# A decoder layer on one core: token blocks loaded and summed between the index logits, the index keys in another buffer, and the second token block's attention scores from halves

## The chip, the core and the metric

The kernel runs on one core of a Trainium2 chip. The core has TensorE (PE, matrix products, with its weight loads shown apart as PEld), VectorE (DVE), ScalarE (ACT), GpSimd (POOL) and SyncE (SP, which issues most DMA transfers). Each engine works through its own instructions in order; semaphores make one wait for another. Products are written to banks of PSUM, a small memory that DVE and ACT read; everything else lies in SBUF. The metric is the device time of one execution in microseconds (us).

## What is computed

One layer: a projection of x into ten parts, retention over four heads, sparse attention over four heads in which an indexer picks the 128 best keys of each query, an output projection with a layer norm, and a gated feed-forward block with another norm. There are 512 tokens and a model width of 1024.

```python
def hybrid_layer(x, positions, w_in, ret_gn_gain, w_out, ...):
    proj = x @ w_in
    rq, rk, rv, rg, aq, ak, av, iq, ik, iw = jnp.split(proj, IN_SPLITS, axis=-1)
    rq = rope(rq); rk = rope(rk); aq = rope(aq); ak = rope(ak); iq = rope(iq); ik = rope(ik)
    ret = silu(rg) * group_norm(retention_chunkwise(rq, rk, rv))
    # indexer: which keys may a query see
    logits = relu(einsum('bqhd,bsd->bqhs', iq, ik))
    score = where(key <= query, einsum('bqh,bqhs->bqs', iw, logits), -inf)
    sel = top_k(score, 128)
    # attention over the chosen keys alone
    s = einsum('bqhd,bkhd->bhqk', aq, ak) * 128 ** -0.5
    att = softmax(where(sel, s, -inf)) @ av
    mix = concatenate([ret, att]) @ w_out
    x = layer_norm(ALPHA * x + mix, ...)
    gate, up = jnp.split(x @ w_gate_up, 2)
    return layer_norm(ALPHA * x + (silu(gate) * up) @ w_down, ...)
```

(Reshapes and chunk loops are left out, and `rope` and the norm are abbreviated.)

## The kernel before

**Numbers in halves.** Most products are made from float32 numbers split into a rounded part of type fp32r and the rest, called hi and lo or h and l. `mm3` (lines 93 to 96) makes hi·hi, hi·lo and lo·hi in three products. `split` makes the parts: ACT casts the hi part (L86), and DVE or POOL subtracts it from the source (L91), or ACT negates it (L88) and a DMA issued by POOL adds the source in memory (L89). Some products are made directly from float32 numbers: transposes, retention's, and the attention scores of the token blocks 0 and 1 (L695).

**Stages.** Tokens lie in four blocks of 128. First the index parts of the projection are made (`acc`), then eight column groups of ak, aq, rk and rq (`proj_feature`, products named `pf`, sixteen of 24 products each), then rv and rg together (`token_pair`), which makes them by seven block products instead of eight. For that it needs sums of blocks of x: block "11" holds the first half of the tokens and the first half of the width, and so on; `x_load` fetches two of these by DMA, `x_sums` forms s3, s1, n2 and s4 by four subtractions and additions on POOL (L394), and `x_split` splits them into halves. Then `proj_token` makes av (products `pt`), with retention beside it. Then `mix_part` makes the output projection (products `mx`), with attention beside it. The feed-forward block comes last.

**Side work.** Beside the products of each stage runs side work that generators deliver: `pace` calls them at a given rate. The list `side` holds, one behind the other, the rotary work of the index parts, the logits (`logits`: two products per head of the indexer, a relu on ACT, L502, and a weighted sum on DVE, L508), and the top-k search (`topk`: 16 times MAX8 and MATCH_REPLACE8 on DVE, L519 and L520, per token block). `both` mixes logits and top-k steps. `slots` runs `mix_part` and, behind each of its sixteen groups of three products, what a plan names for that slot; behind that it steps the side work. `weight()` hands out the next split weight and prepares the one three ahead, so a call of it puts a cast on ACT (`wh`) and a subtraction (`wl`) on DVE or POOL.

**Attention.** `att_score(b)` is a generator of three steps: the scores of four heads, each in a bank of PSUM, and DVE's reading of them, with the mask added and the row maximum taken (L697, L699); then the exponentials on ACT (L702, with the load of ACT's table ahead of the first); then the division by the sum on DVE (L705, L707). `att_tr` transposes the result by PE (L716, tile `apt`) and ACT copies it (L718); `att_pv` multiplies by the values. `ak_split` and `aq_split` make the halves of keys and queries for the blocks 2 and 3; `ak_split` takes a pair of heads at a time. Line 968 makes the scores of block 1 ahead of `mix_part(0, 0)`.

**Buffers.** PSUM has four banks with the tag "d" (`psd`, accumulators) and four with the tag "u" (`psu`, all else: logits, scores, transposes). A new tile of a tag waits until an older one has been read. The large SBUF buffers have tags as well (`s0` to `s10`, `X0` to `X3`), and a new tile of a tag waits for all users of the one before. The index keys `kk3` lie in s8, which the blocks "11" and "22" take after them; rqT lies in s3.

Of the kernel before, what the change touches and what calls it, by code (L numbers as in the profile page):

```python
# [53 lines left out]
def hybrid_layer_kernel(ctx: ExitStack, tc: tile.TileContext, xT, x, pos, w0, wf, wt, wo,  # L54
# [21 lines left out]
    def unit(tag, name, dt=F32):  # L76
        return big.tile([P, 4, S], dt, tag=tag, name=name)
# [142 lines left out]
    def rope(dst, src, ct, st, lo=0, held_back=False):  # L220
        t1 = tmp("rt1")
        t2 = tmp("rt2")
        n = slice(lo, S)
        V.tensor_tensor(t1[:, n], src[:, n], ct[:, n], op=ALU.mult)
        V.tensor_tensor(t2[0:64, n], src[64:128, n], st[64:128, n], op=ALU.mult)
        V.tensor_tensor(t2[64:128, n], src[0:64, n], st[0:64, n], op=ALU.mult)
        if dst is not None:
            late.append(lambda: G.tensor_tensor(dst, t1[:, n], t2[:, n], op=ALU.add))
            if not held_back:
                late.pop()()  # L230
        return t1, t2
# [2 lines left out]
    qa = big.tile([P, 4, M], F32R, tag="s4", name="qa")  # L234
    qb = big.tile([P, 4, M], F32R, tag="s5", name="qb")
    ql = big.tile([P, 4, M], F32R, tag="s6", name="ql")
    kk3 = big.tile([P, 3, S], F32R, tag="s8", name="kk3")
    kh, kl = kk3[:, 0], (kk3[:, 1], kk3[:, 2])
    iwr = tmp("iwr")
    iw = const.tile([P, NB, IH], F32, name="iw")  # L240
# [1 line left out]
    def index_rope():  # L242
        G.memset(kk3[:, 1:].bitcast(F32), 0.0)
        A.activation(iwr, acc0[0], AF.Copy, scale=IDX_SCALE)
        t1, t2 = rope(None, acc0[0], CI, SI)
        ks = tmp("ks")
        V.tensor_tensor(ks, t1, t2, op=ALU.add)
        yield 1.7

        def halves_k():  # L250
            A.copy(kh, ks)
            for b in (0, 64):
                s, d = slice(b, b + 32), slice(b + 32, b + 64)
                G.tensor_tensor(kl[0][s], ks[s], kh[s].bitcast(F32), op=ALU.subtract)
                nc.gpsimd.dma_start(kl[1][d].bitcast(F32), kl[0][s].bitcast(F32))
                nc.gpsimd.dma_start(kh[d].bitcast(F32), kh[s].bitcast(F32))

        def halves_q(i, qs):
            A.copy(qa[:, i], qs[:, P:])
            A.copy(qb[:, i], qs[:, P:])  # L260
            G.tensor_tensor(ql[:, i], qs[:, P:], qa[:, i].bitcast(F32), op=ALU.subtract)
            if i % 2:
                n = slice(i - 1, i + 1)
                for d, s in ((qa[32:64, n], ql[0:32, n]), (qa[96:128, n], ql[64:96, n]),
                             (qb[0:32, n], ql[32:64, n]), (qb[64:96, n], ql[96:128, n])):
                    nc.gpsimd.dma_start(d.bitcast(F32), s.bitcast(F32))

        rounding = halves_k
        for i in range(4):
            t1, t2 = rope(None, acc0[1 + i], CI, SI, P)  # L270
            qs = tmp("qs")
            V.tensor_tensor(qs[:, P:], t1[:, P:], t2[:, P:], op=ALU.add)
            rounding()
            rounding = lambda i=i, qs=qs: halves_q(i, qs)
            yield 2.3
        rounding()
        yield 3.0
        iwp = psu("iwp")
        for j in range(1, NB):
            T.transpose(iwp[:, j * P:(j + 1) * P], iwr[:, j * P:(j + 1) * P], ident)  # L280
        A.copy(iw[:, 1:], iwp.rearrange("p (j c) -> p j c", c=P)[:, 1:, 32:32 + IH])
        yield 3.0
# [36 lines left out]
    akT = unit("s0", "akT")  # L319
    aqT = unit("s1", "aqT")  # L320
    rkT = unit("s2", "rkT")
    rqT = unit("s3", "rqT")
    feats = [akT, aqT, rkT, rqT]
    gnb = const.tile([P, S], F32, name="gnb")

    def const_loads():
# [10 lines left out]
    def dense(items, evac, group=8):  # L337
        for n, item in enumerate(items):
            item()
            if n == 0:  # L340
                settle()
            if n % group == group - 1 or n == len(items) - 1:
                yield
        pending.append(evac)

    def proj_feature(c):
        for i in range(2):
            h, l = weight()
            acc = psd(f"pf{c}_{i}")

            def items(acc=acc, h=h, l=l):
                for kt in range(KT):
                    cs = slice(kt * P, kt * P + P)
                    yield lambda cs=cs, kt=kt: mm3(acc, h[:, cs], l[:, cs], xh[kt], xl[kt], kt == 0, kt == KT - 1)

            yield from dense(list(items()), lambda i=i, acc=acc: rope(feats[c // 2][:, 2 * (c % 2) + i], acc, CT, ST, 0, (c, i) == (7, 1)), 3)

    tok = {}

# [25 lines left out]
    def x_load(tag, *names):  # L385
        t = big.tile([P, 2, 4, T2], F32, tag=tag, name=f"xq{tag}")
        for i, q in enumerate(names):
            tok_half, k_half = int(q[0]) - 1, int(q[1]) - 1
            dma(t[:, i], xT[4 * k_half:4 * k_half + 4, :, T2 * tok_half:T2 * tok_half + T2].rearrange("k p c -> p k c"))
            xq[q] = t[:, i]  # L390
# [134 lines left out]
    def chain(*its):  # L525
        for it in its:
            yield from it
# [44 lines left out]
    def heads(t):  # L572
        return t.rearrange("p (h c) -> p h c", c=P)
# [4 lines left out]
    def ret_score(b):  # L578
        bs = slice(b * P, b * P + P)
        if b:  # L580
            rt["q", b] = tmp(f"rqd{b}")
            G.tensor_tensor(heads(rt["q", b]), rqT[:, :, bs], heads(rt["decay"][:, 1]), op=ALU.mult)
        sc = psu(f"rs{b}")
        for h in range(HEADS):
            T.matmul(sc[:, h * P:h * P + P], lhsT=rkT[:, h, bs], rhs=rqT[:, h, bs], start=True, stop=True)
        rt["s", b] = tmp(f"rst{b}")
        V.tensor_tensor(rt["s", b], sc, rt["decay"][:, 0], op=ALU.mult)

# [67 lines left out]
    def retention():  # L656
        steps = (((ret_keys, 0),), ((ret_score, 0),), ((ret_keys, 1),), ((ret_state, 0),), ((ret_score, 1), (ret_decay, 1)), ((ret_out, 0, 0),),
                 ((ret_out, 0, 1),), ((ret_state, 1),), ((ret_keys, 2),), ((ret_score, 2), (ret_decay, 2)), ((ret_out, 1, 0),),
                 ((ret_out, 1, 1), (ret_scale, 0)), ((ret_state, 2),), ((ret_score, 3), (ret_scale, 1), (gated, 0)), ((ret_out, 2, 0), (ret_gate, 0)),
                 ((ret_out, 2, 1), (gated, 1)), ((ret_out, 3, 0), (gated, 2), (ret_gate, 1)), ((ret_out, 3, 1), (gated, 3)), ((ret_turn, 0), (ret_scale, 2)),  # L660
                 ((ret_gate, 2),), ((ret_turn, 1),), ((ret_scale, 3),), ((ret_gate, 3), (ret_turn, 2)), (), (), ((ret_turn, 3),), ())
        for step in steps:
            for f, *a in step:
                f(*a)
            yield
# [2 lines left out]
    at = {}  # L668
    ak2, aq2 = [], {}

    def ak_split(pair):
        if not ak2:
            ak2.extend(big.tile([P, 4, S], F32R, tag=t, name=f"ak_{t}") for t in ("s7", "s6"))
        hs = slice(2 * pair, 2 * pair + 2)
        A.copy(ak2[0][:, hs], akT[:, hs])
        for h in (2 * pair, 2 * pair + 1):
            G.tensor_tensor(ak2[1][:, h], akT[:, h], ak2[0][:, h].bitcast(F32), op=ALU.subtract)

    def aq_split(b):
        hi, lo = aq2[b] = [tmp(f"aq{i}{b}", F32R) for i in "hl"]  # L680
# [54 lines left out]
    const_loads()  # L735
    tk = chain(*[topk(j) for j in range(1, NB)])

    def x_parts():
        x_load("s8", "11", "22")
        yield 0.01  # L740

    def some(it, n):
        for _ in range(n):
            yield next(it)

    def splits(*a):
        if a[0] == "s4":
            drain(sums_it)
        x_split(*a)
        yield 0.5  # L750

    def x_sums_in():
        next(sums_it)
        next(sums_it)
        yield 0.01

    def both(main, it, every):
        for n, c in enumerate(main):
            yield c
            if n % every == every - 1:  # L760
                yield next(it)

    sums_it = x_sums()
    lg1, lg23 = logits(1), chain(logits(2), logits(3))
    side = chain(index_rope(), lg1, both(lg23, tk, 2), x_parts(), some(tk, 3), x_sums_in(), some(tk, 3), splits("s1", "s4"), some(tk, 1), splits("s4", "s6"), tk)
    run(chain(*[proj_feature(c) for c in range(4)]), pace(side, 1.0))
    x_load("s10", "21", "12")
    run(chain(*[proj_feature(c) for c in range(4, 7)]), pace(side, 1.4))
# [146 lines left out]
    def slots(main, plan, *sides):  # L915
        for n, _ in enumerate(main):
            for f in plan.get(n, ()):
                f()
            for s in sides:
                next(s, None)  # L920
# [15 lines left out]
    def sc_(b):  # L936
        return lambda: next(sc[b])
# [22 lines left out]
    def gate_(n):  # L960
        def f():
# [3 lines left out]
        return f  # L965

    settle()
    sc_(1)()
    slots(mix_part(0, 0), {1: trs_(0, 0), 2: [lambda: ak_split(1)], 6: [lambda: aq_split(2)], 10: [lambda: aq_split(3)], 3: [*trs_(0, 2), *pvs_(0, 0), sc_(1), sc_(1)], 5: pvs_(0, 2), 9: trs_(1, 0),
                           11: [*trs_(1, 2), *pvs_(1, 0)], 13: pvs_(1, 2), 15: [sc_(2)]}, pace(side, 0.5))  # L970
    drain(side)
    slots(mix_part(0, 1), {0: [sc_(2)], 2: [sc_(2)], 3: [sc_(3)], 4: [gate_(0)], 5: trs_(2, 0), 6: [sc_(3)], 7: [*trs_(2, 2), *pvs_(2, 0)],
# [916 lines left out]
```

## Time and profile before

| | |
|---|---|
| median of 3 executions | 606.54 us (606.04 to 606.6) |
| profiled execution | 606.31 us |
| its span, from the first to the last instruction | 604.5 us |
| mean granted clock of TensorE | 0.998 |
| HBM read and written | 90.25 MB and 2.10 MB |

The profile is of one execution, and its rows give start and length in us from the start of the span. A row of the timeline stands for one or several equal instructions (x8) and says in brackets how long the engine sat idle before and which instruction of which engine ended that. The ends of matrix products are modelled and overlap, so their pace is read from start to start. A matrix product of float32 numbers leaves two records.

### The profile page before, as it was taken

The page shows a single profiled execution, that of the slowest core. Times are in us where ns is not written, and L with a number is a line of the kernel's source. Part 1 is how long each engine was busy: PE and PEld are TensorE (multiplying, and loading weights), DVE is VectorE, ACT ScalarE, POOL GpSimd, SP SyncE. Part 2 cuts the span into 40 slices and gives each one's busy share as a digit, 9 for nine tenths or more (in the row PEclk, how much of TensorE's full clock was granted, in tenths as well). Part 3 has the DMA queues.
Part 4 walks back from the last instruction along what each step waited for, and adds up shares of the span by engine and source line. Part 5 has one row for each costly group of instructions (what it writes and reads, how often), then busy time and mean ns, then how long its engine had stood idle before and what let it go on. Part 6 is the DMA issues. An engine that isn't in the chain of part 4 may idle for free.

```text
span 604.5 us, 9142 instructions
## 1 busy us (share of the span) xinstructions
PE 595.5 (99%) x3212; PEld 515.5 (85%) x3212; DVE 528.2 (87%) x975; ACT 367.3 (61%) x640; POOL 196.0 (32%) x196
## 2 busy tenths in 40 slices
PE   9999999999999999999999999999999999999995
PEld 7988888888888888889998888888888888888884
DVE  6896698999958888989998999999999899999856
ACT  5645555445584956777756777777676795547300
POOL 1188323967866400342222222232221021201010
PEclk9999999999999999999999999999999999999999
DMA  8889888699794771696598988988887469678302
GB/s 303 299 217 256 215 208 234 157 240 215 186 225 162 270 266 70 154 227 127 143 274 181 255 191 229 248 198 232 187 224 187 127 189 233 168 243 271 90 36 105
DMA packets 43822, 121.52 MB, mean 201 GB/s; under 512 B 4560, under 2 KB 11536, under 8 KB 38144
## 3 DMA queue, kind: packets, MB, share of 16 engines
q1 hardware_dynamic: 25024, 82.00, 40.2%
q0 software_dynamic: 17872, 36.64, 34.1%
q10 hardware_dynamic: 880, 2.29, 1.2%
q8 instruction: 25, 0.41, 0.3%
q14 instruction: 21, 0.17, 0.1%
HBM read 90.25 MB, written 2.10 MB: 153 GB/s over the span
## 4 chain that ended last, share of the span: by engine, by line
PE 94%; DMA 4%; ACT 1%; issue 1%; DVE 1%; POOL 0%; DVEq 0%; POOLq 0%; ACTq 0%
PE ga L1107 16%; PE gc L1107 8%; PE pf L94 5%; PE pf L95 5%; PE pf L96 5%; PE gb L1107 4%; PE acc L210 4%; PE ga L1097 4%; PE dl L95 2%; PE dl L96 2%; PE dl L94 2%; PE gc L1097 2%; PE dr L95 2%; PE dr L94 2%; PE dr L96 2%; DMA part<-kept 2%
## 5 line engine op out<-in xcount | busy, mean ns | idle before, releaser
L86 ACT CAST wh<-raw 128x1024 fp32r<-128x1024 f32 x49 | 51.2, 1050 | 30.1 <-DMA raw<-in_wt_dram 8.3
L94 PE MATMUL pf<-xh,wh 128*128 128x512 f32 x128 | 50.0, 391 | 0.0
L95 PE MATMUL pf<-xl,wh 128*128 128x512 f32 x128 | 49.9, 390 | 0.0
L96 PE MATMUL pf<-xh,wl 128*128 128x512 f32 x128 | 49.8, 389 | 0.0
L557 POOL TENSOR_TENSOR rs<-ve,half 128x1 f32<-128x1 f32 (+1 forms) x11 | 13.8, 1252 | 74.9 <-DVE ve L556 74.9
L91 DVE TENSOR_TENSOR wl<-raw,wh 128x1024 fp32r<-128x1024 f32 x25 | 32.2, 1297 | 4.3 <-ACT wh L86 4.3
L89 POOL DMA_DIRECT2D wl<-raw x19 | 18.0, 946 | 37.5 <-ACT wl L88 37.3
L96 PEld LDWEIGHTS pf<-xh,wl 128*128 128x128 f32 x128 | 24.0, 188 | 5.1
L95 PEld LDWEIGHTS pf<-xl,wh 128*128 128x128 f32 x128 | 24.1, 188 | 4.7
L94 PEld LDWEIGHTS pf<-xh,wh 128*128 128x128 f32 x128 | 24.0, 188 | 4.6
L519 DVE MAX8 m<-score 128x8 f32<-128x256 f32 (+2 forms) x48 | 26.6, 555 | 0.5
L1012 POOL DMA_DIRECT2D firsts<-in_wgu_dram x18 | 19.7, 1106 | 22.4 <-DMA firsts<-in_wgu_dram 20.2
L520 DVE MATCH_REPLACE8 score<-m,score 128x256 f32<-128x256 f32 (+2 forms) x48 | 26.1, 543 | 0.0
L1144 ACT ACTIVATE gu<-ga 128x512 f32<-128x512 f32 x18 | 10.8, 597 | 25.0 <-PE ga L1107 24.8
L1017 POOL DMA_DIRECT2D graw<-graw x18 | 17.4, 966 | 22.3 <-DVE hu L1163 6.8
L502 ACT ACTIVATE lg<-lg 128x256 f32<-128x256 f32 (+2 forms) x24 | 10.7, 474 | 21.2 <-PE lg L501 21.1
L89 POOL DMA_DIRECT2D slot<-hu x6 | 7.2, 1226 | 41.8 <-ACT slot L88 40.8
L1149 DVE TENSOR_TENSOR gu<-gu,gc 128x512 f32<-128x512 f32 x18 | 12.4, 688 | 9.5 <-ACT gu L1144 9.5
L88 ACT ACTIVATE wl<-raw 128x1024 fp32r<-128x1024 f32 x19 | 20.1, 1059 | 0.0
L508 DVE SCALAR_TENSOR_TENSOR score<-lg,iw,score 128x256 f32<-128x256 f32 (+2 forms) x21 | 12.9, 615 | 7.5 <-ACT lg L502 6.9
L1144 ACT ACTIVATE gt<-ga 128x512 f32<-128x512 f32 (+1 forms) x26 | 13.8, 531 | 6.2 <-PE ga L1097 5.1
L1131 ACT ACTIVATE hu<-hu 128x256 f32<-128x256 f32 x20 | 8.0, 418 | 13.4 <-DVE hu L1121 13.4
(1296 smaller groups left out, 2112.2 us busy)
## 6 DMA issues: line engine op xcount, KB each, us to landing
graw<-in_wgu_dram SPq DMA_DIRECT2D x21, 1024.0 KB, 7.1
wl<-raw POOLq DMA_DIRECT2D x19, 512.0 KB, 7.3
raw<-in_wf_dram SPq DMA_DIRECT2D x8, 1024.0 KB, 7.5
raw<-in_wo_dram SPq DMA_DIRECT2D x8, 1024.0 KB, 5.1
raw<-in_wt_dram SPq DMA_DIRECT2D x6, 1024.0 KB, 5.8
r<-in_wd_dram SPq DMA_DIRECT2D x12, 512.0 KB, 5.9
firsts<-in_wgu_dram SPq DMA_DIRECT2D x18, 256.0 KB, 7.3
firsts<-in_wgu_dram POOLq DMA_DIRECT2D x18, 256.0 KB, 7.8
```

The costliest lines, as they stand in the source:

```text
L86: A.copy(hi, src)
L89: nc.gpsimd.dma_start(lo.bitcast(F32), src, accum_op=ALU.add)
L91: eng_lo.tensor_tensor(lo, src, hi.bitcast(F32), op=ALU.subtract)
L94: T.matmul(acc, lhsT=lh, rhs=rh, start=first, stop=False, **kw)
L95: T.matmul(acc, lhsT=lh, rhs=rl, start=False, stop=False, **kw)
L96: T.matmul(acc, lhsT=ll, rhs=rh, start=False, stop=last, **kw)
L210: T.matmul(acc0[i][:, o:], lhsT=a[:, i * P:i * P + P], rhs=b[kt][:, o:], start=(kt == 0 and p == 0), stop=(kt == KT - 1 and p == 2))
L519: V.max(m8, a)
L520: V.match_replace(out=a, in_to_replace=m8, in_values=a, imm_value=TAKEN)
L1097: T.matmul(gp[n][acc][:, :Q], lhsT=a[:, i * S + k * P:i * S + k * P + P], rhs=parts[q][:, b, k], start=first and j == 0, stop=j == 11, ski ...
L1107: T.matmul(to, lhsT=w[:, o:o + P], rhs=parts[q][:, 0, k] if narrow else parts[q][:, :, k], start=first and not narrow and k == 0, stop=nar ...
L1144: A.activation(gp[n][t], gp[n][acc], AF.Copy, scale=-1.0)
```

## The change

The index keys `kk3` move from buffer s8 to s3. rqT keeps s3, but is now allocated where its first column group is evacuated (`feat(3)`), so that it follows `kk3` there. The blocks "11" and "22" are therefore loaded in the middle of the logits: `both` calls `x_load` behind its sixth step and one of the four sums behind each of the steps 12, 14, 16 and 18. The split of s1 comes two top-k steps earlier.

`ak_split` takes half of the tokens of all heads, where it took all tokens of two heads. `aq_split(1)` is added to retention's list of steps, so the scores of block 1 are made by `mm3` from halves. They move from ahead of `mix_part(0, 0)` into its slot 1, ahead of the transposes there.

```diff
-    kk3 = big.tile([P, 3, S], F32R, tag="s8", name="kk3")
+    kk3 = big.tile([P, 3, S], F32R, tag="s3", name="kk3")
...
-    rqT = unit("s3", "rqT")
-    feats = [akT, aqT, rkT, rqT]
+    feats = [akT, aqT, rkT]
+
+    def feat(j):
+        if j == len(feats):
+            feats.append(unit("s3", "rqT"))
+        return feats[j]
...
-                 ((ret_gate, 2),), ((ret_turn, 1),), ((ret_scale, 3),), ((ret_gate, 3), (ret_turn, 2)), (), (), ((ret_turn, 3),), ())
+                 ((ret_gate, 2),), ((ret_turn, 1),), ((ret_scale, 3),), ((ret_gate, 3), (ret_turn, 2)), ((aq_split, 1),), (), ((ret_turn, 3),), ())
...
-    def ak_split(pair):
+    def ak_split(half_):
         if not ak2:
             ak2.extend(big.tile([P, 4, S], F32R, tag=t, name=f"ak_{t}") for t in ("s7", "s6"))
-        hs = slice(2 * pair, 2 * pair + 2)
-        A.copy(ak2[0][:, hs], akT[:, hs])
-        for h in (2 * pair, 2 * pair + 1):
-            G.tensor_tensor(ak2[1][:, h], akT[:, h], ak2[0][:, h].bitcast(F32), op=ALU.subtract)
+        ks = slice(2 * P * half_, 2 * P * half_ + 2 * P)
+        A.copy(ak2[0][:, :, ks], akT[:, :, ks])
+        for h in (0, 2):
+            src, hi, lo = (t[:, h:h + 2, ks] for t in (akT, *ak2))
+            G.tensor_tensor(lo, src, hi.bitcast(F32), op=ALU.subtract)
...
-    def x_parts():
-        x_load("s8", "11", "22")
-        yield 0.01
-
...
-    def x_sums_in():
-        next(sums_it)
-        next(sums_it)
-        yield 0.01
-
-    def both(main, it, every):
+    def both(main, it):
         for n, c in enumerate(main):
             yield c
-            if n % every == every - 1:
+            if n == 5:
+                x_load("s8", "11", "22")
+            elif n in (11, 13, 15, 17):
+                next(sums_it, None)
+            if n % 2:
                 yield next(it)
...
-    side = chain(index_rope(), lg1, both(lg23, tk, 2), x_parts(), some(tk, 3), x_sums_in(), some(tk, 3), splits("s1", "s4"), some(tk, 1), splits("s4", "s6"), tk)
+    side = chain(index_rope(), lg1, both(lg23, tk), some(tk, 3), splits("s1", "s4"), some(tk, 4), splits("s4", "s6"), tk)
...
     settle()
-    sc_(1)()
-    slots(mix_part(0, 0), {1: trs_(0, 0), 2: [lambda: ak_split(1)], ...
+    slots(mix_part(0, 0), {1: [sc_(1), *trs_(0, 0)], 2: [lambda: ak_split(1)], ...
```

The places where the order changes are these. On TensorE, at the end of `proj_token` (`pt`) and the start of `mix_part(0, 0)` (`mx`), before:

```order
L96 MATMUL pt_1685<-wh_1686,xl_78 128x512
L695 MATMUL as_0_2009<-akT,aqT 128x256
L695 MATMUL as_1_2013<-akT,aqT 128x256
L695 MATMUL as_2_2017<-akT,aqT 128x256
L695 MATMUL as_3_2021<-akT,aqT 128x256
L94 MATMUL mx_0_2026<-wh_1776,mrh 128x512
...
L96 MATMUL mx_1_2027<-wh_1776,mrl 128x512
L716 MATMUL apt_0_2043<-ident,ast 128x128
L716 MATMUL apt_1_2047<-ident,ast 128x128
```

And now:

```order
L94 MATMUL mx_0_2012<-wh_1776,mrh 128x512
...
L96 MATMUL mx_1_2013<-wh_1776,mrl 128x512
L94 MATMUL as_0_2030<-ak_s_1952,aqh_1902 128x256
L95 MATMUL as_0_2030<-ak_s_1953,aqh_1902 128x256
L96 MATMUL as_0_2030<-ak_s_1952,aql_1903 128x256
...
L96 MATMUL as_3_2048<-ak_s_1952,aql_1903 128x256
L722 MATMUL apt_0_2055<-ident,ast 128x128
L722 MATMUL apt_1_2059<-ident,ast 128x128
```

Six `mx` products stood between the scores of block 1 (`as`) and the transposes of block 0 (`apt`, L716, now L722); now they stand ahead of both, and the scores are twelve products. On DVE, at the same place, before:

```order
L707 TENSOR_SCALAR ast<-ast,mx 128x128 x4
L697 ISA ast,mx<-as_0_2009,score 128x256
L697 ISA mx 128x1
...
L699 TENSOR_SCALAR mx<-mx 128x4
L91 TENSOR_TENSOR wl_2031<-raw_1631,wh_2030 128x1024
L519 MAX m_2037<-score 128x8
L520 MATCH_REPLACE score<-m_2037,score 128x512
```

And now (L707 has become L713, L697 L703):

```order
L713 TENSOR_SCALAR ast<-ast,mx 128x128 x4
L91 TENSOR_TENSOR wl_2017<-raw_1631,wh_2016 128x1024
L524 MAX m_2023<-score 128x8
L525 MATCH_REPLACE score<-m_2023,score 128x512
L703 ISA ast,mx<-as_0_2030,score 128x256
L703 ISA mx 128x1
```

The rest of a weight half (`wl`) and a top-k step (MAX, MATCH_REPLACE) stood behind the reading of the scores; now they stand ahead of it. On ACT, ahead of block 0's exponentials, with the engines waited for in brackets, before:

```order
L366 COPY av<-pt_1684 128x512 [waits PE_49]
L702 ACT_TABLE_LOAD
L702 ACTIVATE ast,mx<-ast,mx 128x128 [waits DVE_49]
L702 ACTIVATE ast,mx<-ast,mx 128x128
L702 ACTIVATE ast,mx<-ast,mx 128x128 [waits Activation_49]
```

And now:

```order
L371 COPY av<-pt_1684 128x512 [waits PE_49]
L708 ACT_TABLE_LOAD [waits DVE_49]
L708 ACTIVATE ast,mx<-ast,mx 128x128 [waits Activation_49]
L708 ACTIVATE ast,mx<-ast,mx 128x128 x3
L371 COPY av<-pt_1685 128x512 [waits PE_49]
L86 CAST wh_2016<-raw_1631 128x1024
```

The wait for DVE (for block 0's row maxima, `mx`) stood at the first exponential; now it stands ahead of the table load.

More of the change, by code (lines that the diff above doesn't have):

```diff
@@ L354, in items @@
                     yield lambda cs=cs, kt=kt: mm3(acc, h[:, cs], l[:, cs], xh[kt], xl[kt], kt == 0, kt == KT - 1)
-            yield from dense(list(items()), lambda i=i, acc=acc: rope(feats[c // 2][:, 2 * (c % 2) + i], acc, CT, ST, 0, (c, i) == (7, 1)), 3)
+            yield from dense(list(items()), lambda i=i, acc=acc: rope(feat(c // 2)[:, 2 * (c % 2) + i], acc, CT, ST, 0, (c, i) == (7, 1)), 3)
     tok = {}
@@ L581, in ret_score @@
             rt["q", b] = tmp(f"rqd{b}")
-            G.tensor_tensor(heads(rt["q", b]), rqT[:, :, bs], heads(rt["decay"][:, 1]), op=ALU.mult)
+            G.tensor_tensor(heads(rt["q", b]), feat(3)[:, :, bs], heads(rt["decay"][:, 1]), op=ALU.mult)
         sc = psu(f"rs{b}")
         for h in range(HEADS):
-            T.matmul(sc[:, h * P:h * P + P], lhsT=rkT[:, h, bs], rhs=rqT[:, h, bs], start=True, stop=True)
+            T.matmul(sc[:, h * P:h * P + P], lhsT=rkT[:, h, bs], rhs=feat(3)[:, h, bs], start=True, stop=True)
         rt["s", b] = tmp(f"rst{b}")
@@ L967, in hybrid_layer_kernel @@
     settle()
-    sc_(1)()
-    slots(mix_part(0, 0), {1: trs_(0, 0), 2: [lambda: ak_split(1)], 6: [lambda: aq_split(2)], 10: [lambda: aq_split(3)], 3: [*trs_(0, 2), *pvs_(0, 0), sc_(1), sc_(1)], 5: pvs_(0, 2), 9: trs_(1, 0),
+    slots(mix_part(0, 0), {1: [sc_(1), *trs_(0, 0)], 2: [lambda: ak_split(1)], 6: [lambda: aq_split(2)], 10: [lambda: aq_split(3)], 3: [*trs_(0, 2), *pvs_(0, 0), sc_(1), sc_(1)], 5: pvs_(0, 2), 9: trs_(1, 0),
                            11: [*trs_(1, 2), *pvs_(1, 0)], 13: pvs_(1, 2), 15: [sc_(2)]}, pace(side, 0.5))
```

## The prediction

> **What bounds the kernel now.** I read the page first, then the waits of TensorE alone, then the timeline of the place where the second block's scores stand.
>
> ```profile
> span 604.5 us, 9142 instructions
> PE 595.5 (99%) x3212; PEld 515.5 (85%) x3212; DVE 528.2 (87%) x975; ACT 367.3 (61%) x640; POOL 196.0 (32%) x196
> ```
>
> ```profile
> PE warm L193 <- DVE cold L190: 1.2, 1, 1.2
> PE gb L1097 <- DMA part<-kept: 0.3, 1, 0.3
> PE acc L210 <- ACT xh L201: 0.2, 1, 0.2
> ```
>
> TensorE (PE) is busy in 595.5 of 604.5 us, and the three waits that the whole run lists for it sum to 1.7 us, of which 1.4 us lie at the start. So nothing that becomes earlier on another engine can gain more than 0.3 us in the body of the kernel: a gain has to come out of PE's own work. A wait that is put into PE's stream is another matter. Nothing later has slack to give it back, so it reaches the end in full. That makes two questions: how much PE work goes, and whether PE waits anywhere.
>
> **The first part: loads and sums of the token blocks.** It moves 2 DMA issues (1 MB) on SP from 100.95 us to directly behind the pair at 71.24, four sums on POOL ahead by one or two weight steps, and one split of s1 (a cast on ACT, a subtraction on DVE) by two top-k steps. No instruction is added or removed.
>
> ```profile
> core 0: us, PE busy (x) PEld busy (x) DVE busy (x) ACT busy (x) POOL busy (x), PEclk, DMA share, GB/s
> 90.00:120.00 30.00, 30.00 (x134) 24.82 (x134) 27.54 (x56) 14.31 (x18) 19.69 (x12) 1.00 0.77 202
> ```
>
> ```profile
> 97.58 0.88 POOL L89 DMA_DIRECT2D wl<-raw  x1 [3.94 <-ACT wl L88]
> ...
> 104.40 0.88 POOL L89 DMA_DIRECT2D wl<-raw  x1 [4.61 <-ACT wl L88]
> 105.21 1.39 POOL L228 TENSOR_TENSOR rkT<-rt,rt 128x512 f32<-128x512 f32 x1
> 106.76 4.90 POOL L394 TENSOR_TENSOR xqs<-xqs,xqs 128x1024 f32<-128x1024 f32 x2 [0.16 <-DMA xqs<-in_xT_dram]
> ...
> 112.18 2.71 POOL L394 TENSOR_TENSOR xqs<-xqs 128x1024 f32<-128x1024 f32 x1
> 114.97 3.27 POOL L394 TENSOR_TENSOR xqs<-xqs,xqs 128x1024 f32<-128x1024 f32 x1
> ```
>
> PE is busy in 30.00 of 30.00 us there, so the gain is nothing. For a loss, POOL has to hold something back that PE needs. The first two sums (4.90 us) now stand behind the rotary sum of about 92 to 93.6 us and run to about 98.5, so the weight transfer of 97.58 goes out 1 us later. The other two (5.98 us) follow the next rotary sum, at 98.5 + 0.9 + 1.4 = 100.8, and run to 106.8, so the transfer of 104.40 goes out 2.4 us later.
>
> ```profile
> wl<-raw POOLq DMA_DIRECT2D x19, 512.0 KB, 7.3
> ```
>
> Such a transfer lands in 7.3 us, and a weight half is made three halves ahead of its use, each 24 products of 0.23 us: 16 us, less 2 us for the cast and the negation, less 7.3 us, leaves over 6 us of cover. [...] I take 0. If the cover failed, the whole 4.9 to 6 us of a pair of sums, less that 6, would show: 0 to +3 us. SP comes nearer to its old order after the moved pair, so no later load is put off.
>
> **The second part: scores of block 1.** First the PE price. The old rows are fp32 products, and each is recorded as two.
>
> ```profile
> 200.60 1.89 PE L695 MATMUL as<-akT,aqT 128*128 128x256 f32 x8
> 202.14 0.58 PE L94 MATMUL mx<-wh,mrh 128*128 128x512 f32 x1
> 202.56 0.40 PE L95 MATMUL mx<-wl,mrh 128*128 128x512 f32 x1
> ...
> 203.47 0.39 PE L96 MATMUL mx<-wh,mrl 128*128 128x512 f32 x1
> 203.70 0.64 PE L716 MATMUL apt<-ident,ast 128*128 128x128 f32 x2
> 204.10 0.48 PE L94 MATMUL mx<-wh,mrh 128*128 128x512 f32 x1
> ```
>
> ```profile
> 200.76 1.73 PE as L695 x8
> ...
> 276.31 1.44 PE gb L1097 x12
> ```
>
> These two come from the chain: the old scores take 1.73 us, and twelve products of half operands with the same 256 columns (in the feed-forward stage) take 1.44. So PE's work shrinks by **0.29 us** and no more. The bounds are 1.44 and 2.74 us (12 times the 0.228 us from start to start of 512-column products, (203.47 - 202.56) / 4); I take the 256-column row.
>
> Then the order. PE now runs the first two `mx` products in the place of the scores: from 200.60, six products of 0.228 us, to 201.97. The scores run to 203.41. Directly behind them come the two transposes `apt` of block 0. What these wait for shows in before:
>
> ```profile
> 203.67 0.14 PEld L716 LDWEIGHTS apt<-ident,ast 128*128 128x128 f32 x1 [0.23 <-DVE mx L697]
> ```
>
> Their input `ast` is ready, yet they wait for L697, DVE's reading of the scores of block 1: the four "u" banks hold these scores, and a transpose gets a bank only when one has been read. In before DVE read them at once, and the wait was 0.23 us. Now DVE has three things queued ahead of that reading: the rounding rest `wl` of the next weight half, and a top-k step (MAX, MATCH_REPLACE).
>
> ```profile
> 199.86 0.23 DVE L699 TENSOR_SCALAR mx<-mx 128x4 f32<-128x4 f32 x1
> ...
> 202.40 0.88 DVE L707 TENSOR_SCALAR ast<-ast,mx 128x128 f32<-128x128 f32 x4
> 203.19 0.42 DVE L697 CUSTOM_DVE_ANT_0 ast<-as,score 128x256 f32<-128x256 f32 x1
> ...
> 204.76 1.23 DVE L91 TENSOR_TENSOR wl<-raw,wh 128x1024 fp32r<-128x1024 f32 x1
> 205.91 0.69 DVE L519 MAX8 m<-score 128x8 f32<-128x512 f32 x1
> ...
> 206.71 0.68 DVE L520 MATCH_REPLACE8 score<-m,score 128x512 f32<-128x512 f32 x1
> ```
>
> From the start of `wl` to the end of MATCH_REPLACE8 it is 207.39 - 204.76 = 2.63 us. And `wl` waits for the cast `wh` on ACT:
>
> ```profile
> 199.21 1.28 ACT L702 ACT_TABLE_LOAD   x1
> 200.50 0.40 ACT L702 ACTIVATE ast<-ast,mx 128x128 f32<-128x128 f32 x1
> ...
> 202.06 0.56 ACT L366 COPY av<-pt 128x512 f32<-128x512 f32 x1
> 202.52 1.05 ACT L86 CAST wh<-raw 128x1024 fp32r<-128x1024 f32 x1
> ```
>
> In before that cast ends at 203.57. In the new order the table load waits for DVE's L699 (the wait has moved from the exponential to the load ahead of it). So it starts at 199.86 + 0.23 = 200.09 instead of 199.21, and everything behind it on ACT comes 0.88 us later; the cast ends at 204.45.
>
> The sum, step by step: `wl` starts at 204.48; MATCH_REPLACE8 ends 2.63 later, at 207.11; L697 starts; the transpose's weight load follows 0.48 us after L697's start as in before (203.19 to 203.67), at 207.6; the next `mx` follows 0.43 us after that (203.67 to 204.10), at 208.0. In before it started at 204.10. So PE is **3.9 us late**, after a wait of about 4.2 us (203.41 to 207.6). The 0.29 us saved are inside this: while DVE comes last they are worth nothing.
>
> Behind it everything hangs on PE again: the copies `apts`, the second cast of `ak`, block 1's exponentials and DVE's next reciprocal all follow PE's products in the same order as before, so they shift along. DVE comes out 2.5 us ahead of PE, but no listed wait of PE could use that.
>
> The two new operations for block 1's queries cost nothing, since they fall into idle time:
>
> ```profile
> 194.03 1.05 ACT L86 CAST wh<-raw 128x1024 fp32r<-128x1024 f32 x1 [0.85 <-PE pt L96]
> ...
> 198.78 2.53 POOL L677 TENSOR_TENSOR ak_s<-akT,ak_s 128x512 fp32r<-128x512 f32 x2 [6.14 <-ACT ak_s L675]
> ...
> 209.59 0.62 ACT L682 CAST aqh<-aqT 128x512 fp32r<-128x512 f32 x1
> ...
> 210.29 1.30 POOL L683 TENSOR_TENSOR aql<-aqT,aqh 128x512 fp32r<-128x512 f32 x1 [1.91 <-ACT aqh L682]
> ```
>
> The cast takes 0.62 us in a gap of 0.85, the subtraction 1.30 in a gap of 6.14. Without that cover each would cost at most its length, on engines with 2 us to spare before PE. Splitting the keys by halves of the tokens instead of pairs of heads leaves the sizes the same, and the first half is done at 198.78 + 2.53 = 201.3, before the scores at 201.97.
>
> The profiled execution took 606.31 us, 1.81 more than its span and 0.23 less than the median of 606.54. It becomes 606.31 + 3.9 = 610.2; against the median, 606.54 + 3.9 = **610.4 us**.
>
> **The rivals.**
> *The clock falls during the wait* (chance 0.18). The trace shows the clock falling once, after the last product:
>
> ```profile
> 597.00:604.50 7.50, 0.23 (x2) 0.03 (x1) 4.07 (x8) 0.29 (x1) 0.00 (x0) 0.83 0.32 120
> ```
>
> A mean of 0.83 over 7.5 us is (1 - 0.83) x 7.5 / 0.5 = 2.55 us at half speed, so the fall comes at 601.95, 4.7 us after PE's last work at 597.23. My wait is 4.2 us, a little shorter: it speaks against a fall. The price, from the start of the kernel:
>
> ```profile
> L193 PE MATMUL warm<-cold x9: 407/634/634, 1.2 to 4.6; 128*128 128x512 bf16 x9
> ```
>
> Eight steps of 512 columns take 3.4 us, 0.43 each against 0.23 later. A like stretch of 3.4 us at half speed loses 1.7: 612.1 us, or down to 611.6 where the stretch is partly idle. [...]
>
> *The table load is not held* (0.10): then ACT runs as before, the cast ends at 203.57 and PE is 3.0 us late: 609.5 us. The wait is in the order, against it.
>
> *Not slower* (0.07): the transposes get a bank that is free. Then PE keeps going, loses the old 0.23 us wait and 0.29 us of work and becomes 0.4 us shorter: 606.1. It decides at 203.4: if L697 has read the first scores by then, there is no wait. The row with 0.23 us against DVE's `mx` speaks against it. That the order is not what it seems would be the same case.
>
> *The first part bites* (0.05): +3 us on top, 613.4; it would show as PE waits between 90 and 120 us, where there are none now.
>
> **How the numbers follow.** My forecast has 0.60. The range of 608.9 to 612.6 takes in the forecast with 0.6 us for the pieces of DVE and ACT, the table load and the clock, and leaves out the last two rivals. A measurement here can tell about 0.2%, 1.2 us, from no change. Slower by more than that, above 607.75: forecast, clock, table load and first part, 0.93. Within it: most of the not-slower rival, 0.05. Faster: 0.02.
>
> **What would show it.** In the new profile the waits of PE should list `apt` behind DVE's `mx` of block 1 with about 4 us in all, once, near 203.4; `wl` at 204.5 and the table load at 200.1 confirm the pieces; PE has no new wait from 55 to 200 us; and the end is later by that one wait less 0.3. A granted clock below 1.00 in 205 to 212 us means the clock rival. If `apt` shows no wait I was wrong about the bank; if the wait is there and the end does not move, I was wrong that nothing behind it has slack.

## The result and the profile after

The changed kernel takes **612.35 us** (median of five executions, 611.83 to 612.82) against 606.54 us: ratio 1.0096, 95% interval 1.0085 to 1.0108. The forecast was 610.4 us in a range of 608.9 to 612.6. So it is slower, by 5.8 us where 3.9 were forecast, and within the range, whose upper end had been laid to take in a fall of the clock. The profiled execution took 611.83 us, with a span of 610.0; before, 606.31 and 604.5, so the spans differ by 5.5 us. The head of the page of the changed kernel:

```profile
span 610.0 us, 9155 instructions
PE 596.9 (98%) x3216; PEld 517.2 (85%) x3216; DVE 526.0 (86%) x975; ACT 367.9 (60%) x641; POOL 195.4 (32%) x197
```

PE's work was to shrink by 0.29 us, yet it is busy 1.4 us longer (596.9 against 595.5): some of its products took longer. The waits of PE in the changed kernel (us in total, times, longest):

```profile
PE apt L722 <- DVE mx L703: 4.0, 1, 4.0
PE warm L193 <- DVE cold L190: 1.2, 1, 1.2
PE acc L210 <- ACT xh L201: 0.4, 1, 0.4
PE ga L1097 <- ACT gt L1144: 0.2, 1, 0.2
```

One wait is new, at the first transposes of block 0, for DVE's reading of block 1's scores, and it is 4.0 us long. The old wait for the transfer `part<-kept` is gone. The pieces of the new wait stand in the timelines of the changed kernel (start, length, engine, line); DVE first, then ACT:

```profile
203.28 0.88 DVE L713 TENSOR_SCALAR ast<-ast,mx 128x128 f32<-128x128 f32 x4
204.47 1.22 DVE L91 TENSOR_TENSOR wl<-raw,wh 128x1024 fp32r<-128x1024 f32 x1 [0.32 <-ACT wh L86]
205.62 0.69 DVE L524 MAX8 m<-score 128x8 f32<-128x512 f32 x1
...
206.41 0.68 DVE L525 MATCH_REPLACE8 score<-m,score 128x512 f32<-128x512 f32 x1
207.01 0.41 DVE L703 CUSTOM_DVE_ANT_0 ast<-as,score 128x256 f32<-128x256 f32 x1
```

```profile
200.08 1.28 ACT L708 ACT_TABLE_LOAD   x1 [0.98 <-DVE mx L705]
...
203.40 1.04 ACT L86 CAST wh<-raw 128x1024 fp32r<-128x1024 f32 x1
```

The table load is held by DVE's `mx` and starts at 200.08 (forecast: 200.09); `wl` starts at 204.47 (204.48), and the reading at 207.01 (207.1). PE's timeline shows what the wait does and what follows it:

```profile
203.18 0.28 PE L96 MATMUL as<-ak_s,aql 128*128 128x256 f32 x1
207.49 0.82 PE L722 MATMUL apt<-ident,ast 128*128 128x128 f32 x2 [4.02 <-DVE mx L703]
207.96 0.77 PE L94 MATMUL mx<-wh,mrh 128*128 128x512 f32 x1
208.53 0.63 PE L95 MATMUL mx<-wl,mrh 128*128 128x512 f32 x1
208.96 0.63 PE L96 MATMUL mx<-wh,mrl 128*128 128x512 f32 x1
...
219.80 0.48 PE L94 MATMUL mx<-wh,mrh 128*128 128x512 f32 x1
```

The `mx` behind the transposes starts at 207.96, in before at 204.10: 3.86 us late, as forecast (3.9). But from there the products start 0.43 us apart instead of 0.23. The product of 219.80 stands in the timeline of before at 213.88:

```profile
213.06 1.06 PE L726 MATMUL ao<-apts,av 128*128 128x128 f32 x8
213.88 0.48 PE L94 MATMUL mx<-wh,mrh 128*128 128x512 f32 x1
```

By then PE is 5.92 us late, so the slow stretch cost another 2.06 us. The windows of the changed kernel show it (from:to and length, busy time and number of instructions of PE, PEld, DVE, ACT and POOL, the granted clock, the DMA engines' share, GB/s):

```profile
202.20:205.60 3.40, 1.26 (x11) 1.06 (x9) 2.18 (x6) 2.24 (x7) 0.00 (x0) 1.00 0.97 354
205.60:209.00 3.40, 1.51 (x5) 1.16 (x6) 3.00 (x13) 0.92 (x3) 0.00 (x0) 0.50 1.01 343
209.00:212.40 3.40, 3.40 (x13) 2.81 (x12) 0.00 (x0) 1.78 (x7) 2.50 (x2) 0.50 1.02 369
212.40:215.80 3.40, 3.40 (x18) 2.89 (x17) 2.13 (x8) 3.34 (x10) 0.22 (x1) 1.00 1.01 404
```

The granted clock is at half from 205.6 to 212.4 us and back at full speed behind it. That it fell was a rival in the prediction, not the forecast. It was no accident of one execution: the mean clock was 0.990 or 0.991 in all five, against 0.996 to 0.998 in executions of before. Of 3.86 + 2.06 = 5.92 us the span shows 5.5. The lag falls to 5.7 us at 219 us, where before had a short wait, and to 5.2 at 270 us, where before waited for a transfer that is now in time; then it grows again to 5.5 us, in part where PE now waits 0.2 us for ACT (`ga`). The row of before at 270 us:

```profile
270.39 0.74 PE L1097 MATMUL gb<-part,gb 128*128 128x256 f32 x4 [0.28 <-DMA part<-kept]
```

### The profile page after: what moved, and what is told of

Read it like the earlier page. It is cut to its first block, busy times and chain, and to the rows that moved or that the text cites. A ratio compares the mean times of both kernels' runs of the same rounds, so it can differ in the third digit from the quotient of the medians.

```text
span 610.0 us, 9155 instructions
## 1 busy us (share of the span) xinstructions
PE 596.9 (98%) x3216; PEld 517.2 (85%) x3216; DVE 526.0 (86%) x975; ACT 367.9 (60%) x641; POOL 195.4 (32%) x197
## 4 chain that ended last, share of the span: by engine, by line
PE 94%; DVE 2%; ACT 2%; DMA 1%; issue 0%; DVEq 0%; ACTq 0%
PE ga L1107 16%; PE gc L1107 8%; PE pf L94 5%; PE pf L96 5%; PE pf L95 5%; PE gb L1107 4%; PE acc L210 4%; PE ga L1097 3%; PE mx L94 2%; PE mx L96 2%; PE mx L95 2%; PE dl L94 2%; PE dl L95 2%; PE dl L96 2%; PE dr L96 2%; PE dr L94 2%
```

## The experiments

Two theories to tell apart: (A) the loss is the chain on DVE and ACT in front of the bank's release, plus the clock that falls because PE is idle; (B) the loads and sums, or the products from halves themselves, cost part of it. Then each term of the chain was taken out alone. "Wait" is the wait of PE at `apt` in the profiled execution (for e8 also a second one, at `as`).

| run | wait, us | median, us (executions) | ratio to before, 95% |
|---|---|---|---|
| the change | 4.0 | 612.35 (5) | 1.0096, 1.0085 to 1.0108 |
| e1_first_part | none | 606.42 (12) | 0.9995, 0.9987 to 1.0004 |
| e2_second_part | 4.0 | 612.15 (4) | 1.0089, 1.0075 to 1.0103 |
| e3_scores_first | 1.0 | 607.46 (11) | 1.0008, 0.9997 to 1.0019 |
| e4_topk_later | 2.6 | 610.40 (6) | 1.0058, 1.0045 to 1.0071 |
| e5_table_ahead | 4.0 | 612.28 (4) | 1.0091, 1.0076 to 1.0107 |
| e6_table_and_topk | 2.6 | 610.23 (5) | 1.0062, 1.0050 to 1.0075 |
| e7_scores_first_table | 1.0 | 607.53 (11) | 1.0017, 1.0008 to 1.0025 |
| e8_cover | 0.5 and 0.8 | 608.60 (5) | 1.0032, 1.0019 to 1.0044 |
| e9_table_in_gap | 2.7 | 610.59 (6) | 1.0068, 1.0056 to 1.0081 |
| e10_gap_and_topk | 1.4 | 607.84 (11) | 1.0023, 1.0014 to 1.0031 |
| e11_gap_and_first | none | 606.20 (11) | 0.9993, 0.9984 to 1.0002 |
| e12_filler | 0.8 | 610.63 (6) | 1.0078, 1.0059 to 1.0097 |

Before was measured beside them, with medians of 606.67 (e1 to e4), 606.55 (e5 to e8) and 606.33 us (e9 to e12), and each ratio is to these.

**e1_first_part and e2_second_part: each part alone.** e1 keeps the loads and sums and leaves attention as it was; e2 the other way round.

```diff
 e1, against the changed kernel
-                 ... ((ret_gate, 3), (ret_turn, 2)), ((aq_split, 1),), (), ((ret_turn, 3),), ())
+                 ... ((ret_gate, 3), (ret_turn, 2)), (), (), ((ret_turn, 3),), ())
-    def ak_split(half_):
+    def ak_split(pair):
...
+    sc_(1)()
-    slots(mix_part(0, 0), {1: [sc_(1), *trs_(0, 0)], ...
+    slots(mix_part(0, 0), {1: trs_(0, 0), ...
 e2, against the changed kernel
-    kk3 = big.tile([P, 3, S], F32R, tag="s3", name="kk3")
+    kk3 = big.tile([P, 3, S], F32R, tag="s8", name="kk3")
...
-    side = chain(index_rope(), lg1, both(lg23, tk), some(tk, 3), ...
+    side = chain(index_rope(), lg1, both(lg23, tk, 2), x_parts(), some(tk, 3), x_sums_in(), ...
```

> The first part alone (index keys in s3, the token blocks loaded and summed between the logits); the second part is undone. Theory (the whole loss comes from the transposes' wait in the second part): 606.5 us, within 0.6 of before, no wait of PE between 55 and 200 us, granted clock 0.998. Rival (the first part takes part in the loss, through POOL's sums or the earlier loads): 607.5 us or more, with waits of PE in 90 to 120 us or a longer stretch there.

> The second part alone (scores of block 1 from halves, behind two mx products); the first part is undone. Theory: 612.3 us as with the whole change, one wait of PE of 4.0 to 4.3 us at the transposes, and the clock falls behind it in every execution (0.990). Rival (the first part makes some of the loss): 610.5 us or less.

e1 is level with before, e2 with the whole change. The second part holds all of the loss. Why the first costs nothing shows on POOL in the changed kernel:

```profile
93.22 5.18 POOL L399 TENSOR_TENSOR xqs<-xqs,xqs 128x1024 f32<-128x1024 f32 x2
98.33 0.88 POOL L89 DMA_DIRECT2D wl<-raw  x1
...
105.29 0.89 POOL L89 DMA_DIRECT2D wl<-raw  x1
```

```profile
90.00:120.00 30.00, 30.00 (x134) 24.86 (x133) 27.41 (x61) 15.37 (x19) 21.14 (x15) 1.00 0.72 176
```

The two weight transfers go out at 98.33 and 105.29, which is 0.75 and 0.89 us later than in before (forecast: 1 and 2.4), and PE is still busy for 30.00 of 30.00 us.

**e3_scores_first: the same scores from halves, in their old place.**

```diff
+    sc_(1)()
-    slots(mix_part(0, 0), {1: [sc_(1), *trs_(0, 0)], ...
+    slots(mix_part(0, 0), {1: trs_(0, 0), ...
```

> The whole change, but block 1's scores stand ahead of mix_part again, as in before, still from halves. Theory: DVE reads the scores directly behind block 0's division, at about 204.1 us (the table load stays held, so the division ends at 204.2); the transposes wait 1.2 us instead of 4.2, PE is 1.0 us late there, no fall of the clock, 607.1 us. Rival (products from halves cost more than the fp32 products, whatever the order): 608.5 us or more, with as slower than 1.44 us for its twelve products.

The wait is 1.0 us and the clock does not fall (mean 0.997; before 0.996 to 0.998). So the halves as such are not the loss; their new place is most of it, and about 1 us has another source.

**e4_topk_later: the top-k step comes behind the reading.** The third argument of `pace` is a debt with which the side work starts, so that it comes later.

```diff
-                           ... 13: pvs_(1, 2), 15: [sc_(2)]}, pace(side, 0.5))
+                           ... 13: pvs_(1, 2), 15: [sc_(2)]}, pace(side, 0.5, -0.6))
```

> The whole change, but the top-k step beside the first mx products comes one or two slots later, so that DVE reads the scores directly behind the weight rest. Theory on the wait: it shrinks by the 1.45 us of a top-k step, from 4.2 to 2.7 us, and PE is 2.5 us late: 608.7 us while the clock stays full. [...] Rival: a window in which PE works a third of the time is enough (as the fall 2.3 us after PE's last product in the changed kernel suggests); then it falls in about half of the executions, and these take 1.7 to 2.4 us longer, 610.4 to 611.1 us.

The wait became 2.6 us, shorter by the 1.37 us of MAX8 and MATCH_REPLACE8. On the clock the rival came true: it still fell in the profiled execution, behind 3.4 us in which PE was busy for 39%, but for 3.4 us instead of 6.8 (mean clock 0.993, against 0.990 with the whole change).

**e5_table_ahead, e6_table_and_topk, e7_scores_first_table: the table load out of the chain, first attempt.** A dummy exponential loads the table earlier, alone (e5), with e4 (e6) and with e3 (e7).

```diff
-    ... ((ret_gate, 3), (ret_turn, 2)), ((aq_split, 1),), (), ...
+    ... ((ret_gate, 3), (ret_turn, 2)), ((aq_split, 1), (exp_ahead,)), (), ...
...
+    dummy = const.tile([P, 4], F32, name="dummy")
+    G.memset(dummy, 0.0)
+
+    def exp_ahead():
+        A.activation(dummy, dummy, AF.Exp)
```

> The whole change, with a small exponential of a spare tile in retention's steps, so that ACT's table is loaded long before block 0's exponentials and no longer waits for DVE in front of them. Theory on the wait: ACT comes 1.3 us earlier (0.88 of hold and 0.4 of the load itself), the cast of the weight half ends at 203.1 instead of 204.4, and the wait at the transposes shrinks from 4.2 to 2.9 us; PE is 2.6 us late: 608.7 us at full clock, 610.4 with one stretch of 3.4 us at half clock. Rival (the table load is no part of the wait): 4.2 us of wait and 612.3 us.

> The whole change with both: the table loaded ahead and the top-k step beside the first mx products later. Theory on the wait: the weight rest runs from 203.15 to 204.4, DVE reads the scores behind it, and 1.4 us of wait are left, PE 1.1 us late: 607.3 us. On the clock: a wait of 1.4 us leaves every window of 3.4 us at least 58% busy, above the 39% at which it fell with the shorter wait, so it does not fall: granted clock 0.996 to 0.998. If it falls here as well, 609.0 us.

> The whole change, but block 1's scores stand ahead of mix_part again and the table is loaded ahead. Theory: DVE divides block 0 from 202.0 to 202.8 and reads the scores at 202.75, PE reaches the transposes at 203.3 and hardly waits (0.1 us); what is left is the 0.29 us of products saved and 0.4 us of old waits: 606.0 us, 0.5 to 0.7 below before. Rival (another wait takes the place): 607 us or more, with a wait of PE that the chain names.

All three missed: each took as long as its pair without the early load. ACT's and DVE's timelines of e5 say why:

```profile
193.73 1.28 ACT L677 ACT_TABLE_LOAD   x1
195.02 0.21 ACT L677 ACTIVATE dummy<-dummy 128x4 f32<-128x4 f32 x1
195.13 1.03 ACT L86 CAST wh<-raw 128x1024 fp32r<-128x1024 f32 x1
...
201.47 0.40 ACT L714 ACTIVATE ast<-ast,mx 128x128 f32<-128x128 f32 x1 [2.25 <-DVE mx L711]
```

```profile
199.33 0.28 DVE L709 CUSTOM_DVE_ANT_0 ast<-as,masks 128x128 f32<-128x128 f32 x1
...
200.29 1.09 DVE L711 TENSOR_SCALAR mx<-mx 128x4 f32<-128x4 f32 x1
```

```profile
198.82 2.53 POOL L689 TENSOR_TENSOR ak_s<-akT,ak_s 128x512 fp32r<-128x512 f32 x2 [3.73 <-ACT ak_s L686]
```

The load now stood in front of a cast that DVE waits for, so block 0's scores were read at 199.33 instead of 198.78. Then the scaling of the maxima, four columns wide, took 1.09 us where the changed kernel's took 0.25, and ended at 201.38, just when POOL's second subtraction did (201.35). The exponentials began at 201.47, against 201.38 in the changed kernel: the gain was spent before it arrived. The experiment had not removed the term, it had moved it.

**e8_cover: products into the wait.** e6, with block 0's transposes put off from slot 1 to slot 4 and the rest of attention moved back, so that PE has more `mx` products to work on.

```diff
-    slots(mix_part(0, 0), {1: [sc_(1), *trs_(0, 0)], ... 3: [*trs_(0, 2), *pvs_(0, 0), sc_(1), sc_(1)], 5: pvs_(0, 2), 9: trs_(1, 0),
-                           11: [*trs_(1, 2), *pvs_(1, 0)], 13: pvs_(1, 2), 15: [sc_(2)]}, pace(side, 0.5))
+    slots(mix_part(0, 0), {1: [sc_(1)], ... 4: trs_(0, 0),
+                           6: [lambda: aq_split(2), *trs_(0, 2), *pvs_(0, 0), sc_(1), sc_(1)], 8: pvs_(0, 2), ...
+                           11: trs_(1, 0), 13: [*trs_(1, 2), *pvs_(1, 0)], 14: pvs_(1, 2), 15: [sc_(2)]}, pace(side, 0.5, -0.6))
```

> The whole change with the scores in slot 1, the table loaded ahead and the top-k step later, and the transposes of block 0 three slots later (the rest of block 0 and of block 1 moved behind them in mix_part). Theory (the transposes wait for a bank that DVE frees at 204.7, and products put in between hide it): PE reaches them at 205.4 and does not wait, 606.1 us. Rival (the bank is not the cause, they wait for something that comes with the scores): the wait moves along with them, 607.3 us or more.

A miss by 2.5 us. The time is that of the rival, but its mechanism is not: with nine more `mx` products between the scores and the transposes, the wait there did not move along, it went from 2.6 us (e6) to 0.5. The clock did not fall in the middle (mean 0.998). What came instead is a new wait behind the moved work, at 221.50, at the scores of block 2:

```profile
PE as L94 <- DVE mal L573: 0.8, 1, 0.8
PE apt L728 <- DVE mx L709: 0.5, 1, 0.5
```

The two waits make 1.3 us. The profiled execution was also 0.9 us behind the changed kernel's ahead of this place (a product `pt` at 199.95 us instead of 199.05). The rest was not traced.

**e9_table_in_gap, e10_gap_and_topk, e11_gap_and_first: the table load out of the chain, second attempt.** The dummy exponential goes one place earlier, into 1.57 us in which ACT is idle; alone, with e4's edit and with e3's.

```diff
-    ... ((ret_gate, 3), (ret_turn, 2)), ((aq_split, 1),), (), ...
+    ... ((ret_gate, 3), (exp_ahead,), (ret_turn, 2)), ((aq_split, 1),), (), ...
```

> The whole change with the table of the exponentials loaded early again, but now in ScalarE's idle 1.57 us before the cast mrh at 192.50, where 1.28 us of load and 0.21 us of a dummy Exp on 128x4 fit. In e5 the load stood among the casts, pushed the first wl from 195.1 to 196.2 and the reading of block 0's scores from 198.78 to 199.33, and the scaling of mx then took 1.09 us instead of 0.25 and ended when GpSimd's second subtraction did (201.35). Theory (the load's 1.28 us stands in the chain; e5 missed because its load delayed the casts): exponentials from about 200.1, PE wait at apt 2.6 to 2.9 us instead of 4.0, and as e4 had it with a wait of 2.6 us, 609.6 to 611.1 us, as the clock falls for one window or not at all. Rival (the load was never in the chain, something else holds the exponentials to 201.4): wait 4.0, 612.3.

> e9 and the top-k step behind the reading of block 1's scores. Theory (the two terms add up: 1.28 us of load and 1.37 us of MAX8 with MATCH_REPLACE8 in front of the reading): wait at apt 1.2 to 1.5 us, no fall of the clock, 607.2 to 607.9 us. Rival (the load is not in the chain): as e6, wait 2.6, 610.2.

> e9 with block 1's scores back ahead of the mixing products, as in e3. Theory: e3's wait of 1.0 us (PE idle 1.41 us from start to start) goes but for 0.1 to 0.3 us, and 606.0 to 606.5 us is left: level with the kernel before or 0.1% under it, since the products from halves are 0.29 us shorter and the wait for a transfer of 0.44 us at 270 us is gone. Rival (something else holds the exponentials): 607.5, as e3 and e7.

All three came out as the theory had it. ACT and DVE in e9:

```profile
191.13 1.28 ACT L677 ACT_TABLE_LOAD   x1
192.42 0.20 ACT L677 ACTIVATE dummy<-dummy 128x4 f32<-128x4 f32 x1
192.66 0.59 ACT L572 CAST mrh<-rz 128x512 fp32r<-128x512 f32 x1
...
200.28 0.40 ACT L714 ACTIVATE ast<-ast,mx 128x128 f32<-128x128 f32 x1 [0.99 <-DVE mx L711]
```

```profile
199.93 0.25 DVE L711 TENSOR_SCALAR mx<-mx 128x4 f32<-128x4 f32 x1
...
203.38 1.23 DVE L91 TENSOR_TENSOR wl<-raw,wh 128x1024 fp32r<-128x1024 f32 x1 [0.33 <-ACT wh L86]
```

The load fits into the gap, the scaling is short again, and the exponentials and `wl` start 1.1 us sooner than in the changed kernel, counted from the start of the span (PE is 0.2 us later there, so 1.3 us sooner beside PE's products). The waits then add up like a sum: 4.0, less 1.4 for the top-k step is 2.6, less 1.3 for the load is 2.7, less both is 1.4 (e10), and with the scores first and the load gone nothing is left (e11). e11 does the change's whole computation, and its ratio to before, 0.9993, has 1 in its interval (0.9984 to 1.0002): level, no gain that can be measured.

**e12_filler: more work for PE during the wait.** The three products of block 1's last head are made ten times into the same bank, which gives the same scores and 27 more products.

```diff
-                mm3(sc[:, :n], *(t[:, h * P:h * P + P] for t in aq2[b]), *(t[:, h, :n] for t in ak2), True, True)
+                for _ in range(10 if b == 1 and h == HEADS - 1 else 1):
+                    mm3(sc[:, :n], *(t[:, h * P:h * P + P] for t in aq2[b]), *(t[:, h, :n] for t in ak2), True, True)
```

> The whole change, with the three products of block 1's last head computed ten times instead of once into the same bank (27 more matmuls of 0.118 us, 3.2 us, from 203.4 to about 206.6), so that PE works through most of the wait and the release at apt stays at 207.5. Theory (about 2 us of the loss is the clock, which falls after a window in which PE was mostly idle): the granted clock stays, 0.997 or 0.998, and the time is 610.1 to 610.5 us: more work, and faster by 2 us. Rival (the clock falls for another reason, or its fall costs nothing): 612.3 or more, granted clock 0.990.

PE's timeline in e12:

```profile
206.56 0.28 PE L96 MATMUL as<-ak_s,aql 128*128 128x256 f32 x1
207.65 0.67 PE L723 MATMUL apt<-ident,ast 128*128 128x128 f32 x2 [0.80 <-DVE mx L704]
208.07 0.48 PE L94 MATMUL mx<-wh,mrh 128*128 128x512 f32 x1
208.39 0.39 PE L95 MATMUL mx<-wl,mrh 128*128 128x512 f32 x1
208.62 0.39 PE L96 MATMUL mx<-wh,mrl 128*128 128x512 f32 x1
```

The transposes still start at 207.65, so the wait for the bank is what it was. But the products behind them are 0.23 us apart, the granted clock is 0.998, and the kernel takes 610.63 us: 27 products more than the change and 1.7 us less. Each against the runs of before beside it, the difference is 1.5 us. The two intervals of the ratio overlap (e12's is wide by one execution of 614.20 us, which is open; its other five took 610.13 to 610.88, the change's five 611.83 to 612.82). In the two profiles PE of e12 is 0.16 us later at the transposes, 1.9 us earlier at 212 us and 1.7 us earlier at the end, so the difference arises in the stretch where the changed kernel's clock is at half. The time is close to the forecast's 610.4 us, which was the change without the fall.

## Why the prediction was right, and where it was short

- **PE bounds the body, so a wait put into it reaches the end:** right. Of 5.92 us at 219.80, 5.5 reached the end. That nothing behind had any slack was wrong by 0.4 us, mainly the transfer wait that went away.
- **The loads and sums at nothing:** right (e1), though the second transfer went out 0.89 us later and not 2.4, as the second pair of sums began 0.6 us sooner and took 5.1 us, not 6.0.
- **PE 3.9 us late at the transposes:** right, 3.86 us, and by the pieces named: the held table load at 200.08, `wl` at 204.47, MATCH_REPLACE8 in front of the reading. e4 and e9 took two of the pieces out one at a time, and the wait shrank by 1.4 and 1.3 us, the lengths of these instructions.
- **The 0.29 us of shorter products and the halves of the queries:** hidden, as said. With the wait removed (e11), what is left of the gain lies within the interval around 1. The not-slower rival put this case at 0.4 us less, though its two terms, 0.23 and 0.29, make 0.52; e11 is 0.1 us below its runs of before (606.20 against 606.33).
- **The clock** is the step that failed: the forecast of 610.4 us took it to hold, and it fell in all five executions, so the 3.9 us were 1.9 short. That the time still lies within the range is owed to the room left for this rival. The prediction gave it 0.18, because the one fall in the trace of before came 4.7 us after PE's last product, and a wait of 4.2 us seemed too short. The price was somewhat low (1.2 to 1.7 us on top of 610.4 for one stretch of 3.4 us; it was 6.8 us, the first half partly idle, and 2.06 us in the trace); the condition was wrong. How long PE has been idle does not tell it: the clock fell 4.7 us after PE's last work at the end of before (597.23 to 601.96), but 2.2 us after it at the end of the changed kernel (602.76 to 604.95) and 2.1 us after the last of the scores in the wait (203.46 to 205.59). What fits all three is how much PE worked in the 3.4 us ahead of the fall, 3.4 us being half of the stretch at half clock (205.6 to 212.4). In the wait PE was busy for 1.26 of these 3.40 us, 37%, and the clock fell. The last work of before fills 2.03 of 3.40 us, 60%, and behind it the clock held; it fell behind the next 3.4 us, in which PE did nothing, so the 4.7 us were 1.3 us of the first stretch and the 3.4 of the second.

More such stretches lie at the ends of the kernels and in the waits in the middle. Those of before, of e11 and of e6 in which PE finishes, and the one of e9 with the wait:

```profile
595.20:598.60 3.40, 2.03 (x17) 1.83 (x16) 3.19 (x8) 0.08 (x1) 0.00 (x0) 1.00 0.41 154
```

```profile
595.20:598.50 3.30, 1.53 (x13) 1.33 (x12) 3.10 (x8) 0.29 (x1) 0.00 (x0) 1.00 0.43 159
598.60:601.90 3.30, 0.00 (x0) 0.00 (x0) 2.13 (x4) 0.00 (x0) 0.00 (x0) 1.00 0.24 92
```

```profile
599.50:602.90 3.40, 1.51 (x13) 1.31 (x11) 3.20 (x8) 0.29 (x1) 0.00 (x0) 1.00 0.41 154
602.90:606.30 3.40, 0.00 (x0) 0.00 (x0) 2.11 (x4) 0.00 (x0) 0.00 (x0) 0.50 0.26 100
```

```profile
203.40:206.80 3.40, 0.64 (x5) 0.24 (x4) 3.37 (x9) 0.04 (x1) 0.00 (x0) 1.00 1.01 318
206.80:210.20 3.40, 3.40 (x11) 2.71 (x12) 0.74 (x5) 1.58 (x4) 1.69 (x2) 0.50 1.03 400
```

Behind 60% (before) and 46% (e11, 1.53 of 3.30 us) the clock held for another stretch; behind 44% (e6, 1.51 of 3.40 us) and 19% (e9, 0.64 of 3.40 us) it fell, as it did behind 39% in e4 and behind 36% at the end of the changed kernel (1.22 of 3.41 us). The waits of the table go with it: in the profiled executions no fall in the middle with 1.0 us (e3, mean clock 0.997) and 1.4 us (e10, 0.996; its two stretches with the wait are busy for 2.69 and 2.72 of 3.40 us), a fall with 2.6 us (e4 and e6, 0.993) and 2.7 us (e9, 0.995), and one with 4.0 us (the change, e2 and e5, 0.990). No run has a wait between 1.4 and 2.6 us, so where between them it begins is not shown.

That the early table load is worth 1.3 us only where ACT is idle (e5 against e9) was no step of the prediction. Not tried: a bank of its own for the transposes; by the account above it should take the wait away whatever DVE has queued, but no run shows it. The cast and the subtraction of the weight half (`wl`) were not taken out alone either; e3 and e11, with the scores read ahead of them, are the nearest to it.

## What to carry to other kernels

Before work is moved on the engine that bounds, look which buffer its next instruction needs, who empties it, and what that engine has queued ahead: here two unrelated steps on VectorE and one table load on ScalarE added up to about 4 us, and the top-k step and the load, which were taken out alone, counted at their full length. A wait of TensorE can cost more than its length when the clock falls behind it, as it did here with waits of 2.6 us and more and not with 1.4 us: in the changed kernel 2 us came on top, and products that are thrown away (e12) cost less than the idle array. To take a term out of a chain, put it where its engine is idle; put in front of other work of the same chain, it comes back.

## What the runs showed of the hardware

- The granted clock fell behind stretches of 3.4 us in which PE was still busy for up to 44% (e6). Getting it back took more: the half-clock stretch of 205.6 to 209.0 in the changed kernel, 44% busy (1.51 of 3.40 us), was followed by another half one (so was one of e5, busy for 2.11 of 3.40 us), and the full one of 209.0 to 212.4 by full speed.
- A scaling of 128x4 numbers on VectorE took 1.09 us instead of 0.25 in e5, and likewise in e6, e7 and e8, each time ending within 0.03 us of the end of a subtraction on GpSimd during which it had started. In e8 a second one, at 207.98, took 1.01 us in the same way. The 0.25 us of the changed kernel may be a short case of it: that scaling ended at 200.00, the first of the two subtractions at 199.98; with no subtraction beside it, at 208.50, a scaling took 0.17 us. That the subtraction held the scaling up is the author's reading of these rows; no run here tried it by itself.
- In e7's profiled execution the mean granted clock was 0.947; the other ten had 0.996 to 0.998. It took 608.15 us, the longest of the eleven. Why is open.
